# An encoder layer's instruction order, laid down by the other of the tile layer's two simulators

## Chip, cores and metric

The kernel runs on one core of a Trainium2 chip. The metric is the device time of one execution in microseconds; several runs give a median.

## The reference, cut to what matters

One encoder layer for 1024 tokens of width 2048, in float32. All products below are with weights of 512 to 4096 columns.

```python
def hybrid_layer(x, c, ...):
    mod = jax.nn.silu(c) @ w_ada + b_ada
    shift, scale, gate = jnp.split(mod, 3, axis=-1)
    h = rmsnorm(x, pre_g) * (1.0 + scale[:, None]) + shift[:, None]
    proj = h @ w_in                                   # 2048 -> 4608
    q, k, v, gate_a, u, gate_p = jnp.split(proj, SPLIT_POINTS, axis=-1)
    y_a = windowed_gqa(q, k, v, rel_table, sink) * jax.nn.silu(gate_a)   # 8 heads, blocks of 128, window 128
    y_p = multiscale_pool(u, w_pool_grp, pool_scale) * jax.nn.silu(gate_p)
    g = jax.nn.sigmoid(h @ w_merge + b_merge)         # 2048 -> 4096
    g_a, g_p = jnp.split(g, 2, axis=-1)
    merged = g_a * (y_a @ w_br_attn) + g_p * (y_p @ w_br_pool)
    o = merged @ w_out
    return x + gate[:, None] * rmsnorm(o, post_g)
```

## The kernel before

**Products.** Every large product is a Strassen scheme in Winograd's form: seven products of half-size blocks in place of eight. Each float32 operand is split into a rounded part and a remainder (`split`, L95 and L96: ScalarE writes the high part, VectorE the low one), and a product of two split operands is three matmuls (high by high, high by low, low by high). The moving operands, named `B11, T3, T2, B21, T4, T1, B22`, are made once from the activations and stay in SBUF for a whole pass: 7 names, 4 parts of the inner dimension, high and low, which is 56 tiles of 128x512, and the pool `big` has 56 slots. The weights come by DMA in pairs of 128 columns (`raw`, L187, four slots), are combined and split into rings of four (`whi`, `wlo`), and are used at once. The core of one product, in the function `strassen`:

```python
def product(wts, mov, ps, fresh=False):
    hi, lo = wts
    for n, (w_, m_) in enumerate(((hi, 0), (hi, 1), (lo, 0))):
        for i, j in enumerate(js):
            nc.tensor.matmul(ps, w_[:, i], op[mov][j][m_], ...)      # L235
```

A pair of weights goes through seven such products into three PSUM banks: X (with B11, then B21), V (T3, then T4) and Z (T2, T1, B22; it begins with a copy of X). With four parts of the inner dimension a product is 12 matmuls of 128x512 and a pair 84. Between the products ScalarE and VectorE read the banks (`u2` and `p7` at L245, `u4` at L290, additions at L102 and L105), and results go to DRAM (L311).

**Stages.**
1. Start: x and the first weights of the conditioning `w_ada` are loaded; rows are normalised and transposed by matmuls (`XT`, L405, with `turn`, L397), the shift and scale columns come from small matmuls (`GEMV`, L453). A first short set of pairs (the ramp) runs while the inner dimension's first half is still being made ready.
2. Pass 1: 34 pairs of `w_in` and `w_merge` for the first half of the inner dimension; partial sums go to `part_d`. Beside it run the rest of the conditioning (VectorE, L470), sums of the blocks of `w_out` (`weight_sums`, stored in `ws_d`), and the second half of h: rows of x (`xt`, L738 and L739) are scaled on ScalarE and transposed by matmuls (L745).
3. Pass 2: the same 34 pairs for the second half, with partial sums read back; results in `proj_d`. Beside it runs the attention in steps for 8 heads and 8 blocks of queries, two heads a step: scores (L849 to L851), softmax (L855 to L862), transposes (`PT`, L872) one step behind, values (`PV`, L882 to L884) two steps behind, gates at L836. Then the pooling branch (L928 to L976).
4. The branch products: 8 pairs for the attention branch, 8 for the pooling branch, with the gates (`gt`, L1074) and the sums of the two branches.
5. The output product (`out_pair`, matmuls at L1134 to L1136), in two halves of the tokens by two of the columns, and the final normalisation and residual (L1144 to L1156).

**Order.** The statements are traced by Python in one order: `run` steps through a pair's generator and puts steps of the side work between the products by hand (lists such as `every=(0, 2, 4, 6)`). The tile layer then makes the program. While it simulates the program, each engine takes, whenever it is free in the simulation, the earliest-written statement that is ready there, and slots of the pools are handed out as that goes on. That gives one list of instructions for each engine and for each queue of DMA issues (nearly all on SP's), with semaphores between them; on the chip each list runs in order. A few statements are tied to what was traced before them on their engine, by `tc.keep_in_program_order` (`keep`, and `pin` in `split`), and small writes to fresh slots (`claim`, L512) reserve them early.

## Time and profile before

| | us |
|---|---|
| median of 3 runs | 2147.35 (2147.01 to 2148.66) |
| the profiled execution | 2151.69 |
| its span, first to last instruction | 2149.9 |
| TensorE busy | 2100.2 |
| TensorE weight loads busy (beside the matmuls) | 1717.1 |
| VectorE busy | 1537.6 |
| ScalarE busy | 1129.0 |

The mean granted TensorE clock over the span is 0.996. Times inside the profile are microseconds from the first instruction. A busy time of TensorE counts matmuls that overlap in its pipeline once. L235 is line 235 of the kernel; a line can be that of a helper that many callers use, so operations are told apart by the names of the tiles.

### The profile page before, as it was taken

The page shows a single profiled execution, that of the slowest core. Times are in us where ns is not written, and L with a number is a line of the kernel's source. Part 1 is how long each engine was busy: PE and PEld are TensorE (multiplying, and loading weights), DVE is VectorE, ACT ScalarE, POOL GpSimd, SP SyncE. Part 2 cuts the span into 40 slices and gives each one's busy share as a digit, 9 for nine tenths or more (in the row PEclk, how much of TensorE's full clock was granted, in tenths as well). Part 3 has the DMA queues.
Part 4 walks back from the last instruction along what each step waited for, and adds up shares of the span by engine and source line. Part 5 has one row for each costly group of instructions (what it writes and reads, how often), then busy time and mean ns, then how long its engine had stood idle before and what let it go on. Part 6 is the DMA issues. An engine that isn't in the chain of part 4 may idle for free.

```text
span 2149.9 us, 28954 instructions
## 1 busy us (share of the span) xinstructions
PE 2100.2 (98%) x9567; PEld 1717.1 (80%) x9567; DVE 1537.6 (72%) x2754; ACT 1129.0 (53%) x2124; POOL 7.4 (0%) x66
## 2 busy tenths in 40 slices
PE   6999999999989999999999999999999999999998
PEld 3588888887878888888888888888788887878886
DVE  5786666786546676777776778666957967879667
ACT  5654444443464546767765433333645644667654
POOL 0000000000000000000000000000000000000000
PEclk9999999999999999999999999999999999999999
DMA  9986566998666446446454766765745655696997
GB/s 328 288 278 202 188 206 206 303 322 270 226 213 201 129 166 209 156 156 199 147 164 157 235 210 208 236 197 163 234 164 177 214 177 166 200 302 220 299 312 243
DMA packets 303255, 466.11 MB, mean 217 GB/s; under 512 B 23882, under 2 KB 144866, under 8 KB 303104
## 3 DMA queue, kind: packets, MB, share of 16 engines
q1 hardware_dynamic: 301648, 462.02, 66.0%
q0 software_dynamic: 1120, 2.19, 0.3%
q8 instruction: 75, 1.23, 0.2%
q14 instruction: 76, 0.62, 0.1%
q10 hardware_dynamic: 336, 0.06, 0.0%
HBM read 340.41 MB, written 125.85 MB: 217 GB/s over the span
## 4 chain that ended last, share of the span: by engine, by line
PE 85%; DMA 6%; DVE 5%; ACT 1%; issue 1%; SPq 0%; ACTq 0%; DVEq 0%; POOLq 0%
PE Z L235 29%; PE V L235 19%; PE X L235 19%; PE Z L1134 2%; PE Z L1135 2%; PE Z L1136 2%; PE V L1136 1%; PE V L1134 1%; PE V L1135 1%; PE GEMV L453 1%; DMA raw<-in_w_merge_dram 1%; DVE wlo L96 1%; PE X L1136 1%; PE X L1135 1%; PE X L1134 1%
## 5 line engine op out<-in xcount | busy, mean ns | idle before, releaser
L95 ACT ACTIVATE whi<-raw 128x512 fp32r<-128x512 f32 (+1 forms) x528 | 320.0, 609 | 501.4 <-PE Z L235 263.1
L96 DVE TENSOR_TENSOR wlo<-raw,whi 128x512 fp32r<-128x512 f32 (+1 forms) x528 | 346.6, 662 | 195.1 <-PE Z L235 119.2
L96 DVE TENSOR_TENSOR wlo<-wr,whi 128x512 fp32r<-128x512 f32 x224 | 151.1, 689 | 60.4 <-ACT whi L95 55.2
L95 ACT ACTIVATE whi<-wr 128x512 fp32r<-128x512 f32 x224 | 138.6, 629 | 92.5 <-DVE wlo L96 35.7
L102 DVE TENSOR_TENSOR raw<-raw,raw 128x512 f32<-128x512 f32 x80 | 55.2, 690 | 95.8 <-DMA raw<-in_w_merge_dram 71.1
L1074 ACT ACTIVATE gt<-gt,cols 128x512 f32<-128x512 f32 x64 | 45.9, 722 | 101.1 <-DMA gt<-proj_d 81.8
L235 PE MATMUL V<-T3h,whi 128*128 128x512 f32 x336 | 92.2, 393 | 3.9 <-DVE u L102 3.9
L235 PE MATMUL Z<-B22h,whi 128*128 128x512 f32 x336 | 93.8, 398 | 1.2 <-ACT u L290 1.2
L235 PE MATMUL X<-B11h,whi 128*128 128x512 f32 x336 | 92.4, 393 | 2.3 <-DVE part L102 1.0
L235 PE MATMUL Z<-T1h,whi 128*128 128x512 f32 x336 | 91.9, 392 | 0.9 <-ACT T1h L95 0.9
L235 PE MATMUL Z<-T2h,whi 128*128 128x512 f32 x336 | 92.3, 394 | 0.0
L235 PE MATMUL V<-T4h,whi 128*128 128x512 f32 x336 | 92.3, 393 | 0.0
L235 PE MATMUL Z<-B22l,whi 128*128 128x512 f32 x336 | 91.8, 393 | 0.0
L235 PE MATMUL Z<-T2l,whi 128*128 128x512 f32 x336 | 91.5, 393 | 0.0
L235 PE MATMUL X<-B11l,whi 128*128 128x512 f32 x336 | 91.3, 390 | 0.2 <-DVE B11l L96 0.2
L235 PE MATMUL Z<-B22h,wlo 128*128 128x512 f32 x336 | 91.4, 392 | 0.0
L235 PE MATMUL X<-B21h,whi 128*128 128x512 f32 x336 | 90.9, 390 | 0.0
L235 PE MATMUL V<-T4l,whi 128*128 128x512 f32 x336 | 90.9, 390 | 0.0
L235 PE MATMUL Z<-T1l,whi 128*128 128x512 f32 x336 | 90.8, 390 | 0.0
L235 PE MATMUL V<-T3l,whi 128*128 128x512 f32 x336 | 90.8, 390 | 0.0
L235 PE MATMUL Z<-T2h,wlo 128*128 128x512 f32 x336 | 90.8, 390 | 0.0
L235 PE MATMUL V<-T4h,wlo 128*128 128x512 f32 x336 | 90.8, 390 | 0.0
(306 smaller groups left out, 4848.2 us busy)
## 6 DMA issues: line engine op xcount, KB each, us to landing
part<-part_d SPq DMA_DIRECT2D x136, 256.0 KB, 5.0
ada<-in_w_ada_dram SPq DMA_DIRECT2D x128, 256.0 KB, 4.4
raw<-in_w_in_dram SPq DMA_DIRECT2D x64, 512.0 KB, 4.1
raw<-in_w_merge_dram SPq DMA_DIRECT2D x64, 512.0 KB, 5.6
wr<-ws_dS SPq DMA_DIRECT2D x64, 512.0 KB, 5.4
wr<-in_w_out_dram SPq DMA_DIRECT2D x48, 512.0 KB, 5.1
proj_d<-part SPq DMA_DIRECT2D x68, 256.0 KB, 2.2
sw<-in_w_out_dram SPq DMA_DIRECT2D x64, 256.0 KB, 5.1
```

The lines of the kernel that those rows point to most:

```text
L95: ins = (nc.scalar.activation(hi, src, AF.Copy), nc.vector.tensor_tensor(lo, src, f32(hi), ALU.subtract))
L96: nc.vector.tensor_tensor(lo, src, f32(hi), ALU.subtract))
L102: return (eng or nc.vector).tensor_tensor(o, a, b, ALU.add)
L235: nc.tensor.matmul(ps, w_[:, i], op[mov][j][m_], start=fresh and i == 0 and n == 0, stop=i == nj - 1 and n == 2, skip_group_check=True)
L453: ins = nc.tensor.matmul(pv[g:g + 32, :], scz[:, kc, :], tile_of(kc), start=kc < 4, stop=kc >= 12, tile_position=(0, g))
L1074: nc.scalar.activation(gt, gt, AF.Sigmoid, bias=cols[:, col:col + 1])
L1134: nc.tensor.matmul(pb, hi, w[0], start=first, stop=False, skip_group_check=True)
L1135: nc.tensor.matmul(pb, lo, w[0], start=False, stop=False, skip_group_check=True)
L1136: nc.tensor.matmul(pb, hi, w[1], start=False, stop=last, skip_group_check=True)
```

## The change

The tile context gets one more argument. Without it, the layer's scheduler decides which statement is ready by running the program in its plain simulator; with it, in its detailed timeline simulator, which follows the parts of an engine and the transfers as separate devices. Statements, tiles, pools, buffer counts and ties are the same.

```diff
     args.append(nc.dram_tensor("out_0_dram", (1, S, D), F32, kind="ExternalOutput").ap())
-    with tile.TileContext(nc) as tc:
+    with tile.TileContext(nc, schedule_with_timeline_sim=True) as tc:
         encoder_layer(tc, *args)
```

## The prediction

> **What bounds the kernel now.** I read the first two parts of the page first: which engine has no time left, and where.
>
> ```profile
> span 2149.9 us, 28954 instructions
> ...
> PE 2100.2 (98%) x9567; PEld 1717.1 (80%) x9567; DVE 1537.6 (72%) x2754; ACT 1129.0 (53%) x2124; POOL 7.4 (0%) x66
> ```
>
> TensorE (PE) is busy for 2100.2 of 2149.9 us, no other engine for more than 1537.6. So all that another order of the same instructions can win is 2149.9 - 2100.2 = 49.7 us of idle time, and what PE loses at a lower clock. The windows view says where these lie (columns: stretch, length, busy us of each engine with instructions in brackets, granted clock, DMA share, GB/s).
>
> ```profile
> 0.00:100.00 100.00, 78.89 (x387) 44.00 (x387) 62.28 (x156) 54.94 (x120) 3.94 (x46) 1.00 0.95 310
> 600.00:700.00 100.00, 94.20 (x433) 77.42 (x432) 57.63 (x92) 56.20 (x133) 0.00 (x0) 0.97 0.69 220
> 700.00:800.00 100.00, 100.00 (x443) 82.66 (x442) 72.23 (x116) 51.85 (x90) 0.00 (x0) 1.00 0.44 145
> 1500.00:1600.00 100.00, 98.61 (x431) 80.08 (x430) 80.79 (x130) 59.85 (x102) 0.00 (x0) 1.00 0.61 200
> 1600.00:1700.00 100.00, 100.00 (x441) 82.23 (x440) 77.11 (x123) 60.91 (x107) 0.00 (x0) 1.00 0.52 168
> 1800.00:1900.00 100.00, 96.44 (x410) 78.50 (x409) 80.65 (x129) 62.77 (x114) 0.00 (x0) 0.97 0.66 217
> 1900.00:2000.00 100.00, 98.71 (x433) 80.89 (x434) 85.25 (x145) 71.80 (x139) 0.00 (x0) 1.00 0.77 246
> 2100.00:2149.90 49.90, 40.96 (x181) 33.43 (x179) 36.34 (x63) 23.25 (x49) 0.00 (x0) 0.95 0.69 235
> ```
>
> The first stretch holds 100 - 78.89 = 21.1 us of the idle time, with the DMA engines at 0.95: that is the load of x and of the conditioning weights. The last holds 49.9 - 40.96 = 8.9 us, the final normalisation behind the last product. The 2000 us between hold the rest, 49.7 - 21.1 - 8.9 = 19.7 us, and half of that lies in two stretches, 600:700 (5.8) and 1800:1900 (3.6), the only two of these rows between the ends with a clock under 1. The PE rows of the waits view name the causes (columns: us in total, times, longest); these four hold 13 of the 19.7 us.
>
> ```profile
> PE b L745 <- ACT xt L739: 5.8, 2, 4.2
> PE V L235 <- DVE u L102: 3.9, 3, 1.7
> PE X L1134 <- DVE c L1085: 2.3, 1, 2.3
> ...
> PE PV L883 <- DVE pp L96: 1.0, 2, 0.6
> ```
>
> **What the change touches.** No instruction, size or buffer count changes. The tile layer lays down, before the run, the order of each engine's instructions: it simulates the program, and whenever an engine of the simulation is free, the earliest-written statement that is ready there goes next; slots of the pools are handed out in the same order. The chip then executes each engine's list strictly in that order. The change replaces the simulation that decides what is "ready". So each term below is an order that comes out otherwise, and I price it by what good and bad orders cost in the trace of before. Which orders come out can't be read from that trace; that is the main unknown.
>
> **The steady part: nothing.** Two products of the same name in successive weight pairs:
>
> ```profile
> 215.51 1.07 PE L235 MATMUL Z<-B22h,whi 128*128 128x512 f32 x4
> ...
> 234.55 1.07 PE L235 MATMUL Z<-B22h,whi 128*128 128x512 f32 x4
> ```
>
> They are 19.04 us apart; a pair is 7 products of 12 matmuls, so a matmul costs 19.04 / 84 = 0.2267 us and a product 2.72 us, without a wait. The split weights stand in rings of four (whi, wlo), the raw ones in four slots, so whoever schedules can't run far ahead and need not. How much disorder this absorbs is shown where it failed:
>
> ```profile
> 507.18 7.47 DMA raw<-in_w_merge_dram
> ...
> 515.99 5.28 DMA raw<-in_w_merge_dram
> ...
> 524.04 3.02 PE V L235 x12
> ```
>
> Here (the chain of waits) VectorE's list twice stood behind a weight load, 12.8 us together, and PE lost at most the 1.7 us of the longest "V <- DVE u" wait. So a wrong order on VectorE costs PE almost nothing until it blocks for about 12.8 - 1.7 = 11 us. I cost reordering of DVE, ACT and the SP queue inside the passes at zero; the cover is the rings of four, and without it every blocked us would be PE's.
>
> **The places without cover.** Two places show what PE pays when its own list has something too early (timeline of PE):
>
> ```profile
> 636.99 1.07 PE L235 MATMUL Z<-B22h,wlo 128*128 128x512 f32 x4
> 642.23 1.12 PE L745 MATMUL b<-ident,xt 128*128 128x128 f32 x4 [4.17 <-ACT xt L739]
> 643.00 2.06 PE L235 MATMUL Z<-T2h,whi 128*128 128x512 f32 x4
> ...
> 647.66 1.08 PE L235 MATMUL X<-B21h,whi 128*128 128x512 f32 x4
> ```
>
> From 636.99 to 647.66 are 10.67 us. The work in them is 16 matmuls of 0.2267 us, 3.63, and four transposes; the transposes take about 0.40 us at full rate (an estimate: 642.23 to 643.00, 0.77, at the rate seen there, 2.06 for four matmuls against 1.08). The loss is 10.67 - 3.63 - 0.40 = 6.6 us: 4.17 of waiting, 2.5 of a slower clock behind it. After the shorter wait at 524 the 12 matmuls took 3.02 against 2.72 us: no half rate. The Trainium skill ("TensorE: Matmul & The Clock Gate", Part 1) says the clock falls to half after an idle window of some 3.4 us and needs about as long a busy one to return; the trace agrees in kind (4.17 us did it, 1.7 did not), and by its figures the slow stretch would add an estimated 1.7 us instead of 2.5.
>
> ```profile
> 1822.45 1.07 PE L235 MATMUL Z<-T1h,wlo 128*128 128x512 f32 x4
> 1825.81 0.47 PE L1134 MATMUL X<-whi,mh 128*128 128x512 f32 x1 [2.29 <-DVE c L1085]
> ...
> 1828.59 2.08 PE L235 MATMUL Z<-B22h,whi 128*128 128x512 f32 x4 [0.56 <-ACT u L290]
> ...
> 1833.87 0.63 PE L1135 MATMUL X<-whi,ml 128*128 128x512 f32 x1
> ```
>
> Here the first matmuls of the output product (L1134) stand ahead of the last product of the branch (L235), and their bank is not free. From 1822.45 to 1833.87 are 11.42 us for 4 + 4 + 12 = 20 matmuls (four of L1134 to L1136 lie between the shown rows), 4.5 us at 0.2267: a loss of 6.9. So one entry that comes too early in PE's list costs about 7 us.
>
> Now the count. The stall at 642 comes from a load that landed later than the order supposed; a simulation that follows the transfers in more detail should put these transposes later: -6.6 us. The one at 1825 is a bank handed over by VectorE, no transfer; I leave it (0, at best -6.9). Against that stand four other handovers, at which the 56 slots of "big" pass from one moving operand to the next: into pass 2, into each branch, and between the halves of the output product. For the first three the view of the tile B11h gives the time of the first and last write.
>
> ```profile
> L95 ACT ACTIVATE B11h<-y x8: 614/616/635, 1496.5 to 1657.4; 128x512 fp32r<-128x512 f32 x8
> ...
> L95 ACT ACTIVATE B11h<-h x4: 615/619/634, 734.8 to 739.7; 128x512 fp32r<-128x512 f32 x4
> ```
>
> Pass 2 starts to fill at 734.8 us, the first branch at 1496.5, the second ends its first group at 1657.4; the fourth lies in 1900:2000. Each statement there takes a freed slot in the order in which the simulation finds it ready, and slots given to a later group keep an earlier one waiting. The windows 700:800, 1500:1600, 1600:1700 and 1900:2000 show that today they cost PE at most 0.00, 1.4, 0.00 and 1.3 us: there is little to win, and 6.6 us each to lose. Bounds for one: 0 (the order comes out alike), and 13.2 (two such stalls, head and tail of the handover). I take the middle, 6.6, the nearest measured stall: 4 x 6.6 = +26.4 us.
>
> The start: I take 0. DMA at 0.95 sets it; a 512 KB weight load moved ahead of x costs 0.5 MB / 310 GB/s = 1.7 us (an estimate from the first window), the order may win as much: -5 to +5 us for three of them. The tail: 0, bounds -2 and +4 (the 8.9 us are one chain behind the last product).
>
> Sum: -6.6 + 26.4 = +19.8 us. Against the profiled execution's 2151.69 us that is 2171.5; that one lay 4.3 us above the median of the runs, 2147.35, so the forecast is 2147.35 + 19.8 = **2167.2 us**. A difference of 0.2%, 4.3 us, is about what a measurement of this kernel can tell from none.
>
> **The rivals.** *Faster: the detailed simulation orders better.* One mechanism: entries that came too early go where their inputs have landed. Both 7 us stalls go (-6.6 - 6.9) and the stall at 524 (-1.7), the handovers stay free: 2147.35 - 15.2 = 2132.2. With the first alone it is 2140.8. For it: the three largest mid-span losses are of this kind. Against it: it can't win more than the 19.7 us of idle time and the slow clock of two windows, 2 x 100 x (1 - 0.97) = 6 us, so not reach below 2122. It decides as long as at most one of the four handovers comes out worse, since each that does gives back 6.6 us. Chance 0.26.
>
> *Much slower: the attention stage.* Behind the first pairs of pass 2, PE's list holds, between the products, the scores, transposes and values of 8 heads times 8 blocks, each behind a chain over ScalarE and VectorE.
>
> ```profile
> L836 ACT ACT_TABLE_LOAD x13 | 16.7, 1283 | 4.4 <-DMA g<-proj_d 4.2
> ```
>
> ScalarE loads a table for the gates 13 times here, 16.7 us, and must load the one of the softmax back each time; of these loads the detailed simulator by its own source takes no account. If it supposes these chains shorter than they are, PE's entries come too early, each time. PE's two waits for such a chain in the PV row are 0.5 us each; at two per block and head that is 64 x 2 x 0.5 = 64 us: with the 19.8 it is 2231.2. Against it: the transposes lag a step and the values two behind the scores in the statements, which the readiness rule doesn't shorten. Chance 0.18.
>
> *No change: both simulations find the same things ready.* The steady part, which is nearly all of PE's list, can't tell them apart; if the handovers come out alike too, it stays at 2147. Chance 0.09.
>
> **How the numbers follow.** The forecast (one to eight misplaced entries, 2152 to 2200) has 0.47, the attention rival 0.18 (2200 to 2250 and more), no change 0.09, faster 0.26. So slower has 0.65, same 0.09, faster 0.26. The range reaches from 2134, which leaves out the faster rival's best cases, a chance of about 0.1, to 2235, where the attention rival's upper half begins, about 0.09. The likeliest case's own range is 2152 to 2200.
>
> **What would show it.** In the profile after: PE busy us and instructions unchanged (2100 within some us, 9567), the pitch of 19.04 us kept in the passes; the difference is all in PE's idle time and in windows with a clock under 1. Right on the first term: no wait of "b L745 <- ACT xt" over 2 us. Right on the second: waits of 2 to 5 us on L235 or L1134 for splits (L95, L96) near the four handovers, windows there with 5 to 10 us less PE. The attention rival shows as many short waits on L849, L872 and L882 to L884. I am wrong if the steady passes themselves show gaps (then the rings aren't the cover I take them for), if the first 100 us move by more than 5 us, or if PE's busy time grows without idle time.

## The result and the profile after

| | before | after |
|---|---|---|
| median of 6 runs each, us | 2150.33 (2147.01 to 2154.39) | 2160.93 (2156.99 to 2163.40) |
| ratio of after to before | | 1.0049, 95% interval 1.0036 to 1.0061 |
| profiled execution / span, us | 2151.69 / 2149.9 | 2161.23 / 2159.4 |

The kernel is 10.6 us slower; 19.8 was forecast. The span grew by 9.5 us. The first lines of the page of after:

```profile
span 2159.4 us, 29009 instructions
...
PE 2105.6 (98%) x9567; PEld 1716.3 (79%) x9567; DVE 1534.0 (71%) x2754; ACT 1115.7 (52%) x2114; POOL 7.4 (0%) x66
```

TensorE runs the same 9567 matmuls and is busy 5.4 us longer (2100.2 before); its idle time grew by only 4.1 us, from 49.7 to 53.8. The windows view of after, for the stretches that the prediction showed (length, then busy us of PE, PEld, DVE, ACT, POOL, then granted clock, DMA share, GB/s):

```profile
0.00:100.00 100.00, 80.45 (x363) 41.50 (x363) 59.34 (x149) 52.34 (x114) 3.91 (x46) 1.00 0.95 311
600.00:700.00 100.00, 98.09 (x462) 80.48 (x462) 55.33 (x90) 60.06 (x147) 0.00 (x0) 1.00 0.69 216
700.00:800.00 100.00, 99.18 (x438) 81.83 (x437) 75.31 (x122) 52.70 (x91) 0.00 (x0) 1.00 0.48 156
1500.00:1600.00 100.00, 99.30 (x436) 81.35 (x436) 81.12 (x132) 60.19 (x102) 0.00 (x0) 1.00 0.61 205
1600.00:1700.00 100.00, 96.84 (x426) 79.56 (x425) 75.04 (x122) 59.72 (x102) 0.00 (x0) 1.00 0.48 161
1800.00:1900.00 100.00, 99.35 (x437) 81.52 (x436) 81.64 (x130) 63.26 (x114) 0.00 (x0) 1.00 0.68 221
1900.00:2000.00 100.00, 97.25 (x428) 79.90 (x427) 85.27 (x142) 72.11 (x139) 0.00 (x0) 1.00 0.72 240
2100.00:2159.40 59.40, 47.50 (x205) 37.80 (x203) 40.29 (x70) 26.80 (x57) 0.00 (x0) 0.93 0.64 220
```

The two weak stretches of before, 600:700 and 1800:1900, are mended: PE 98.09 and 99.35, clock 1.00. New are 1600:1700, where PE was full and now has 96.84, and the first row, where PE is busier (80.45 against 78.89) with fewer matmuls done (363 against 387). Of the PE rows of the waits view of after, behind those of the start (in us: total, times, longest):

```profile
PE V L235 <- DVE u L102: 4.0, 1, 4.0
PE Z L1134 <- ACT u L1216: 4.0, 4, 1.5
...
PE PT L872 <- DVE g L887: 2.3, 1, 2.3
PE V L235 <- ACT p L245: 2.1, 1, 2.1
...
PE b L745 <- ACT xt L739: 1.4, 2, 1.0
```

To see where the time came from I count the matmuls of the large products (L235 and L1134 to L1136; 8400 in both traces) and compare when the same number of them had started. The counts begin at 0, and the last row runs from the start of the last of these matmuls. At the chosen counts the work beside them is the same too. The last column holds the same stretch in the profiles of other kernels of the study whose lists there are as in before or as in after.

| stretch, by count of product matmuls | before, us | after, us | difference | other profiles with these lists |
|---|---|---|---|---|
| start to 120 (ramp) | 105.7 | 110.7 | +5.0 | before 104.8 to 106.0; after 110.2 |
| 120 to 1760 (pass 1, first half) | 376.0 | 382.8 | +6.8 | before 376.0 to 377.3; after 380.6 to 381.8 |
| 1760 to 2480 (pass 1, second half) | 188.3 | 180.8 | -7.5 | before 186.6 to 189.1; after 179.9 to 182.5 |
| 2480 to 3000 (into pass 2) | 118.0 | 119.0 | +1.0 | the same |
| 3000 to 5280 (attention, pooling) | 631.1 | 632.9 | +1.8 | before 628.0 to 634.9; after 634.3 to 635.3 |
| 5280 to 6360 (first branch) | 247.5 | 246.3 | -1.2 | before 247.6 to 248.0; after 246.4 to 246.6 |
| 6360 to 6960 (second branch) | 137.8 | 139.8 | +2.0 | before 137.6 to 139.2; after 141.0 to 141.1 |
| 6960 to 7160 (branch to output) | 52.7 | 46.6 | -6.1 | before 52.9 to 53.2; after 47.3 to 50.3 |
| 7160 to 8400 (output) | 283.6 | 289.1 | +5.5 | before 283.0 to 285.7; after 290.3 to 291.6 |
| last matmul to the end | 9.3 | 11.4 | +2.1 | before 9.1 to 9.7; after 11.3 to 11.4 |

The column of differences adds up to 9.5 with unrounded numbers. The change is thus ten differences of both signs, none over 8 us. "Loss" below means: in a stretch, the sum of the times from one matmul's start to the next, less the median of such steps of the same kind.

### The profile page after: what moved, and what is told of

It is laid out like the page before. It is cut to its first block, busy times and chain, and to the rows that moved or that the text cites. A ratio compares the mean times of both kernels' runs of the same rounds, so it can differ in the third digit from the quotient of the medians.

```text
span 2159.4 us, 29009 instructions
## 1 busy us (share of the span) xinstructions
PE 2105.6 (98%) x9567; PEld 1716.3 (79%) x9567; DVE 1534.0 (71%) x2754; ACT 1115.7 (52%) x2114; POOL 7.4 (0%) x66
## 4 chain that ended last, share of the span: by engine, by line
PE 82%; DMA 9%; DVE 5%; ACT 1%; issue 1%; SPq 0%; DVEq 0%; ACTq 0%; POOLq 0%
PE Z L235 27%; PE V L235 18%; PE X L235 18%; DMA xt<-in_x_dram 2%; PE Z L1134 2%; DMA raw<-in_w_merge_dram 2%; PE Z L1135 2%; PE Z L1136 2%; PE X L1134 1%; DVE wlo L96 1%; PE X L1135 1%; PE X L1136 1%; PE V L1136 1%; PE V L1135 1%; PE V L1134 1%
## 5 line engine op out<-in xcount | busy, mean ns | idle before, releaser
L96 DVE TENSOR_TENSOR wlo<-raw,whi 128x512 fp32r<-128x512 f32 (+1 forms) x528 | 347.7, 662 | 150.7 <-PE Z L235 96.1
L96 DVE TENSOR_TENSOR wlo<-wr,whi 128x512 fp32r<-128x512 f32 x224 | 150.2, 689 | 66.6 <-ACT whi L95 62.8
L102 DVE TENSOR_TENSOR raw<-raw,raw 128x512 f32<-128x512 f32 x80 | 55.3, 691 | 96.0 <-DMA raw<-in_w_merge_dram 64.4
L235 PE MATMUL V<-T3h,whi 128*128 128x512 f32 x336 | 93.4, 395 | 4.4 <-DVE u L102 4.0
L105 DVE TENSOR_TENSOR ws<-raw 128x512 f32<-128x512 f32 (+1 forms) x88 | 58.6, 666 | 54.1 <-DMA raw<-in_w_merge_dram 40.7
L235 PE MATMUL V<-T4h,whi 128*128 128x512 f32 x336 | 93.3, 393 | 2.1 <-ACT p L245 2.1
L235 PE MATMUL Z<-T1h,whi 128*128 128x512 f32 x336 | 91.9, 392 | 1.6 <-ACT u L245 1.6
L235 PE MATMUL V<-T3h,wlo 128*128 128x512 f32 x336 | 93.3, 394 | 0.0
L235 PE MATMUL V<-T3l,whi 128*128 128x512 f32 x336 | 93.1, 394 | 0.0
L235 PE MATMUL X<-B11h,whi 128*128 128x512 f32 x336 | 92.0, 392 | 1.0 <-DVE part L102 1.0
L235 PE MATMUL Z<-T1l,whi 128*128 128x512 f32 x336 | 92.0, 391 | 0.7 <-DVE T1l L96 0.7
L235 PE MATMUL Z<-B22h,whi 128*128 128x512 f32 x336 | 91.6, 392 | 1.1 <-ACT u L290 1.1
L235 PE MATMUL Z<-T1h,wlo 128*128 128x512 f32 x336 | 92.6, 391 | 0.0
L235 PE MATMUL X<-B21h,wlo 128*128 128x512 f32 x336 | 91.9, 390 | 0.0
L235 PE MATMUL Z<-T2h,wlo 128*128 128x512 f32 x336 | 91.9, 391 | 0.0
L235 PE MATMUL Z<-B22l,whi 128*128 128x512 f32 x336 | 91.9, 390 | 0.0
L235 PE MATMUL Z<-T2h,whi 128*128 128x512 f32 x336 | 91.9, 391 | 0.0
L235 PE MATMUL X<-B21h,whi 128*128 128x512 f32 x336 | 91.7, 390 | 0.0
L235 PE MATMUL Z<-T2l,whi 128*128 128x512 f32 x336 | 91.7, 390 | 0.0
L235 PE MATMUL Z<-B22h,wlo 128*128 128x512 f32 x336 | 91.5, 390 | 0.0
```

The source lines that it names most:

```text
L96: nc.vector.tensor_tensor(lo, src, f32(hi), ALU.subtract))
L102: return (eng or nc.vector).tensor_tensor(o, a, b, ALU.add)
L105: return nc.vector.tensor_tensor(o, a, b, ALU.subtract)
L235: nc.tensor.matmul(ps, w_[:, i], op[mov][j][m_], start=fresh and i == 0 and n == 0, stop=i == nj - 1 and n == 2, skip_group_check=True)
```

## The experiments

Theory: the difference is a sum of single places where an engine's list came out in another order, and each can be undone almost alone. Rival: the detailed order is slower as a whole, so that what is mended in one place comes back in another. "Tied" means an ordering on one engine without a wait on the chip (`add_manual_dep` of the kind NoSync). Each kernel was timed beside the kernel before, on the same chip; its ratio is to that. An edit makes the scheduler lay the lists anew, so each moves more than the entry meant: of TensorE's 9567 matmuls, about 3100 stand elsewhere with the tie of pass 1 on after and 403 with the same tie on before, and 5 to 292 with each other single edit.

**The ramp: conditioning products by fours.** Each of the 64 products of L453 uses 32 of TensorE's columns and leaves two matmul records (128 in both traces), so x2 below is one of them; the counts in the first expectation are of records. Timeline of PE in before:

```profile
77.26 1.05 PE L453 MATMUL GEMV<-ada,scz 128*32 128x512 f32 x4
...
79.84 1.05 PE L453 MATMUL GEMV<-ada,scz 128*32 128x512 f32 x4
```

and in after, where a product of the ramp is put between the two:

```profile
77.53 1.04 PE L453 MATMUL GEMV<-ada,scz 128*32 128x512 f32 x2
78.50 0.50 PE L235 MATMUL V<-T3h,wlo 128*128 128x512 f32 x1
78.94 1.04 PE L453 MATMUL GEMV<-ada,scz 128*32 128x512 f32 x2
```

Two side by side take 1.05 us, one alone 1.04. First edit, on after:

```diff
-            for kc in (2 * q, 2 * q + 1):
+            for kc in range(4 * q, 4 * q + 4) if pin else (2 * q, 2 * q + 1):
```

> The kernel after, with the conditioning products of the start (L453) written four to a step instead of two, so that four of 32 columns stand together in TensorE's list. Theory (the cost of the change is a sum of local entries of the lists): in after they stand two at a time, 1.04 us for two; in before four at a time, 1.05 us for four. Each group of four closed up saves about 1 us of TensorE's time, and the ramp up to 105 us gets back the 5 us that it lost: about -5 us in all, TensorE's busy time down by about as much, nothing else moved. Rival (the load sets the start): the DMA engines are at 0.95 of their time in the first 100 us, so TensorE would wait for weights instead: 0 us, busy time down by 5 us and idle time up by 5 us.

Measured: 2162.71 us, ratio 1.0050 (1.0032 to 1.0068): as after. Product 120 came at 109.95 us, and between 58 and 110 us ten groups still were x2: the scheduler went on giving each of the four its place as its own weights were ready. So the edit did not bring about what it was to test, and decides nothing. The second edit issues the four from the last loaded tile down:

```diff
+            for kc, tk in [(k, tile_of(k)) for k in range(4 * q, 4 * q + 4)][::-1] if pin else ...:
-                ins = nc.tensor.matmul(pv[g:g + 32, :], scz[:, kc, :], tile_of(kc), ...)
+                ins = nc.tensor.matmul(pv[g:g + 32, :], scz[:, kc, :], tk, ...)
```

> The kernel after with the conditioning products in fours, each four issued from the last loaded tile down, so that the first of a four waits for its last weights and the four stand together in TensorE's list (in the run with ascending order they had still come in twos). Theory (groups of four of 32 columns run side by side, groups of two take as long): about 8 pairs of 1 us saved between 70 and 100 us, the 40th to 120th product of pass 1 comes 4 to 5 us earlier, -4 us in all. Rival (the weights' arrival sets the ramp): the 120th product stays at 110 us within 1 us, 0 in all.

Measured: 2151.45 us, ratio 1.0005 (0.9991 to 1.0019), the time of before. From 69 us on the groups are fours; timeline of PE:

```profile
79.81 1.06 PE L453 MATMUL GEMV<-ada,scz 128*32 128x512 f32 x8
80.81 0.73 PE L235 MATMUL X<-B21h,whi 128*128 128x512 f32 x2
```

Product 120 starts at 99.1 us, 11.6 us earlier than in after. That is over twice the expectation, since fours also beat before's pairs. In its profile, which at 2156.81 us is a slow sample of this kernel, some of it is lost again at the end of the branches (stretch 6960 to 7160, 50.3 us against 46.6) and in the output. The rival falls: although the DMA engines are at 0.95 of their time there, TensorE's own work set the ramp. The busy time of L453 up to 110 us was 31.1 us in before, 37.7 in after and 25.7 here. The large products even start earlier in after, at 49.2 us with 22 conditioning products done, against 55.3 with 30 done in before; but from there to product 120 it is 61.5 us instead of 50.3.

**Pass 1: VectorE behind a weight load.** The chain of waits of after:

```profile
460.67 10.21 DMA raw<-in_w_merge_dram
...
470.98 0.69 DVE ws L105
471.67 0.61 DVE u L102
...
472.32 5.49 PE V L235 x12
```

VectorE's list has the first difference of the next pair (`ws`) ahead of the addition that frees bank V (`u`). From its issue the load took 10.21 us; VectorE stood for the last 5.10 of them, TensorE waited 4.0 us, and the next 12 matmuls took 5.49 us instead of 2.72. Edit, on after and on before:

```diff
-            sub(s3, a11, a21)
+            behind_v(sub(s3, a11, a21))
...
```

Here `behind_v` ties its instruction behind the latest addition out of bank V.

> The kernel after, with VectorE's first difference of the next weight pair (L260) put behind the addition that frees bank V. Theory (local): the wait of 4.0 us on V <- DVE u at 472 us and the half clock behind it, 7.2 us together, go: -7 us, 2154. Rival 1 (the load is late whatever the order): the weights that VectorE stood for took 10.21 us, and TensorE waits for the next pair's first product instead: 0 to -2 us. Rival 2 (the order as a whole is worse, not single entries): the list changes in many other places too, and new stalls of the same kind come up elsewhere: within 3 us of the kernel after, with the stall at 472 gone.

> The kernel before with VectorE's first difference of the next weight pair (L260) put behind the addition that frees bank V. Theory (the wait V <- DVE u is in before too: 1.5 us at 501 in its own profile, 4.4 to 5.3 us in other runs with the same order there, and 2 us at 522): no loss over 1 us at 495 to 530, -3 to -6 us in the median, 2147, and the runs scatter less than before's 2147 to 2160. Rival (the load behind it is late in any case): the wait moves to the split of the next pair and the time stays within 2 us.

On after: 2156.56 us, ratio 1.0024 (1.0012 to 1.0037), 4.4 us less than after by the medians and 5.4 by the ratios, between the theory and the second rival. The stall is gone; from product 120 to product 2480 pass 1 takes 556.3 us against 563.6, -7.3. In its profile 2.8 us of that go at the first branch (stretch 5280 to 6360) and 2.5 in the output, the first in lists that the tie changed, the second in lists that it did not. After's own profile also had the largest stall: the three other profiles with after's order at this place lost 5.0, 5.2 and 6.0 us there, about what the runs gained. On before: 2152.43 us, ratio 1.0005 (0.9993 to 1.0017), no gain: the rival's time. Nor do the runs scatter clearly less (12 runs from 2148.84 to 2157.44; before, 27 from 2145.35 to 2157.47). In its profile no loss between 495 and 530 us is left, and pass 1 takes 560.9 us where four profiles with before's lists take 562.9 to 565.2; of these 2 to 4 us the median shows nothing. So the local theory holds at its place in both kernels, but in the second its worth is not shown.

These runs also show how much luck is in one profile. VectorE's and SP's lists of this part are the same in before and in the three kernels below that differ from it at the handover near 1825 us. The loss at about 501 us was 1.5, 5.3, 4.9 and 6.3 us, as the load came. Before's own profile had the smallest.

**Output: two token rows apart.** The last matmuls of each output product are written for the first 128 tokens, then for the second. In after the two are interleaved to the end, so that both banks come free at once. ScalarE in before (timeline):

```profile
1897.54 0.60 ACT L1216 ACTIVATE u<-Z 128x512 f32<-128x512 f32 x1 [0.95 <-PE Z L1136]
1898.03 1.27 ACT L95 ACTIVATE whi<-wr 128x512 fp32r<-128x512 f32 x2
1899.21 0.58 ACT L1216 ACTIVATE u<-Z 128x512 f32<-128x512 f32 x1
```

ScalarE and TensorE in after:

```profile
1900.53 1.15 ACT L95 ACTIVATE whi<-wr 128x512 fp32r<-128x512 f32 x2 [1.76 <-PE Z L1136]
1901.59 1.07 ACT L1216 ACTIVATE u<-Z 128x512 f32<-128x512 f32 x2
```

```profile
1902.22 0.50 PE L1134 MATMUL Z<-whi,mh 128*128 128x512 f32 x1 [1.47 <-ACT u L1216]
```

Before copies the first row's bank under the second row's matmuls; after copies both at the end, and TensorE waits. Edit, on after: the first of the second row's last matmuls tied behind the last of the first row's, and likewise in the last product of all.

> The kernel after, with the second token row's last matmuls of each output product (L1134) tied behind the first row's last one, in the last product of all its matmuls. Theory (local): the four waits of Z <- ACT u (L1216), 4.0 us together, go, since ScalarE copies the first row's bank beside the second row's matmuls, and the tail behind the last matmul goes from 11.4 to 9.3 us: -6 us, 2155. Rival (the splits set the pace there): TensorE needs all the splits of a product sooner and waits for them (L95) instead: -2 us from the tail alone, or 0.

Measured: 2157.80 us, ratio 1.0026 (1.0012 to 1.0040). The gain against after is 3.1 us by the medians and 4.9 by the ratios; with intervals this wide it can be the 6 us of the theory or the 2 us of the rival. The tail is 8.7 us instead of 11.4, and no wait of Z for `u` (L1216) is left. In the middle part both theories have some right: waits for splits appeared (2.1 us of Z <- ACT whi, 1.4 of Z <- DVE wlo), and this profile's output stretch, 289.2 us, is no shorter than after's 289.1, though three other profiles of after's lists have 290.3 to 291.6. How much the middle part gains stays open.

**The transposes.** On before, each written a side step later:

```diff
-        if n >= 2:
-            turn_x((n - 2) // 2, n % 2, held.pop(n - 2))
+        if n >= 3:
+            turn_x((n - 3) // 2, (n - 3) % 2, held.pop(n - 3))
...
```

> The kernel before with the transposes of x for the scores (L745) written one side step later. Theory (they came too early for the load that they stand behind): no wait of b <- xt over 1 us, the losses at 598 to 617 and 622 to 647 us, 9.4 us together, fall to the 3.3 us that they are in after: -6 us, 2144.5. Rival (the load sets the pair, and another wait takes the place): the loss stays above 6 us, -3 us at most.

Measured: 2144.56 us, ratio 0.9966 (0.9953 to 0.9978), -7.3 us. The row "PE b L745 <- ACT xt" is no longer among its waits, and the two losses are 0.5 us each, less than after's 3.3 together. The mechanism that the prediction gave for this place is shown.

**The loss at 1825 us, three ways.** The prediction put it down to output matmuls that stand too early in TensorE's list. First edit, on before: the first output matmul tied behind the branch's last, its first split behind the branch's last split.

> The kernel before, with the first matmul of the output product (L1134) tied behind the last one of the branch (L235) and its first split behind the branch's last split; 18 lines of TensorE's list move, 8 of ScalarE's. Theory (one entry that comes too early in TensorE's list, with the slow clock behind it): the whole loss at 1825 us goes, -6.5 to -6.9 us, 2143.5. Rival (only the wait of 2.3 us hangs on the order, the low clock of that window on something else): -2.3 us, 2148, with the four matmuls of 2.08 us still there.

Measured: 2152.46 us, ratio 0.9999 (0.9985 to 1.0013). The loss there is 8.0 us instead of 7.3: both theories fall. TensorE now waits 5.5 us for the copy `u` of L290 in one piece. In before, ScalarE's timeline tells why:

```profile
1821.29 0.72 ACT L1074 ACTIVATE gt<-gt,cols 128x512 f32<-128x512 f32 x1 [3.53 <-DMA gt<-proj_d]
1821.92 1.13 ACT L95 ACTIVATE mh<-m 128x512 fp32r<-128x512 f32 x2
...
1826.90 0.63 ACT L95 ACTIVATE mh<-m 128x512 fp32r<-128x512 f32 x1 [2.80 <-DVE m L102]
1827.43 0.61 ACT L95 ACTIVATE whi<-wr 128x512 fp32r<-128x512 f32 x1
1827.95 0.58 ACT L290 ACTIVATE u<-Z 128x512 f32<-128x512 f32 x1
```

The sigmoid of a gate that only the last block needs holds ScalarE for 3.53 us; VectorE's sums wait for the splits behind it, the next split for those sums, and the copy for that split. Second edit: the first one, and the last split of the output operand written behind the copy.

> The kernel before with the tie of the run before (output matmuls behind the branch's last product), and besides with the last split of the output operand (L95, mh) written behind the copy of bank Z (L290), so that this copy no longer stands behind a split that waits for VectorE's sums on ScalarE. Theory now (the loss at 1825 us comes from ScalarE's list: the copy u <- Z of L290 waits behind mh <- m, that behind sums on VectorE, these behind a gate load of L1074): the copy comes at about 1824.5 instead of 1828, the loss there falls from 7.3 us (8.0 in the run before) to about 1.7, -5.5 us against the kernel before, 2145. Rival (the gate's load alone sets it, since it holds up ScalarE whatever stands behind it): 4 us or more stay lost, at most -3 us.

Measured: 2152.13 us, ratio 1.0003 (0.9994 to 1.0011). At the copy the loss fell to 2.0 us as the theory said, but 5.6 us were lost at 1830 to 1840, on VectorE's backlog (X <- DVE wlo, L96): 7.6 together. Third edit, on before alone: that gate's sigmoid issued behind the copy of L290.

> The kernel before with one gate moved: the sigmoid of the last block of the second branch (L1074) is issued behind the copy of bank Z (L290) instead of as soon as its load should be there. Theory (the loss at 1825 us begins with this sigmoid, which stands in ScalarE's list 3.5 us before its load has landed and holds up the splits of the output operand, the copy of bank Z and VectorE's sums behind them): the loss at 1823 to 1840 us, 7.3 us in before and 7.6 to 8.0 in the two runs that only moved what stands behind the gate, falls to 2 us or less: -5.5 us, 2146.5. Rival (VectorE's sums are late by themselves): another wait takes the place as in those two runs, 5 us or more stay lost.

Measured: 2147.03 us, ratio 0.9989 (0.9975 to 1.0004). Losses 2.1 and 1.4 us, 3.6 together; the stretch 6960 to 7160 takes 49.2 us against 52.7. In this profile half of the loss went with the gate; by the runs the gain is 2.4 us, and its interval holds 0. ScalarE's list of this kernel has a wait of 4.04 us for VectorE's sums at 1829 in its place. After has the gate in the same order too (a wait of 2.74 us), but 16 output matmuls ahead of the branch's last product, where before has four and the first edit none; the losses are 0.8 (up to 3.8 in other profiles of after's lists), 7.3 and 8.0 us. By that comparison, what the prediction called a matmul that comes too early is the filling of the gap, and there was too little of it. No edit changed the number of these matmuls alone, so this is argued and not shown.

**All together.** On after: the tie, the rows, the fours; and on both kernels the edits that had looked good.

> The kernel after with three edits together: the first difference behind the addition that frees bank V, the two token rows of the output products apart, the conditioning products in fours. Theory (the difference between the kernels is a sum of such entries): -4.4 of the first as measured, -3 of the second as measured, -4 of the third as expected: 2149.5, the time of before, within 3 us. Rival (each edit makes the scheduler lay other stalls elsewhere): 2155 or more.

> The kernel before with the tie of the difference, the transposes a step later and the last gate late. If the plain order's losses are single entries they add up: -7.5 as measured for the transposes, -3 to -6 for the tie, -5.5 for the gate: 2134. If the scheduler lays other stalls instead: 2142 or more.

> The kernel after with the three edits of the run that came to 2139.7, and the last gate late. There the loss at 1813 to 1829 is 1.3 us, so a gain of at most 1 us is to be expected if losses are local: 2139. If moving the gate lays stalls elsewhere: 2142 or more.

| kernel | median, us | ratio to before |
|---|---|---|
| after with tie, rows, fours | 2139.67 | 0.9947 (0.9934 to 0.9961) |
| the same and the last gate late | 2139.82 | 0.9951 (0.9934 to 0.9968) |
| before with tie, transposes, last gate late | 2142.56 | 0.9960 (0.9945 to 0.9976) |

The three edits on after gave 21.3 us by the medians; alone, by their ratios against 1.0049, they gave 5.4, 4.9 and 9.5, or 19.8. So on after, within what the intervals can tell, single entries do add up, and the version is about 12 us faster than before. The late gate added nothing to it (at most 1 us was expected). The page of the first:

```profile
span 2135.5 us, 28961 instructions
...
PE 2091.8 (98%) x9567; PEld 1715.0 (80%) x9567; DVE 1526.3 (71%) x2754; ACT 1107.8 (52%) x2120; POOL 7.4 (0%) x66
```

On before the run came out on the other branch of its expectation, 2142.6 instead of 2134, but because the parts were overrated: alone they measured +1.1 (tie), -7.3 (transposes) and -2.4 us (gate) by their ratios, -8.6 together, and 0.9960 is -8.6. The intervals of the two kinds overlap: with a few entries put right, neither simulator's order is shown to be the better one.

## Why the prediction was right or wrong

The direction, and the size within a factor of two, came out; of the terms, few did, and the direction was luck.

- **Steady passes, 0.** The pitch held (timeline of PE in after):

```profile
220.45 1.07 PE L235 MATMUL Z<-B22h,whi 128*128 128x512 f32 x4
239.49 1.07 PE L235 MATMUL Z<-B22h,whi 128*128 128x512 f32 x4
```

  19.04 us as before. But one gap of 7.2 us opened at 468 to 478, the sign that the prediction named as against it. The step that failed is the cover of about 11 us. The 12.8 us from which it was worked out are the lengths of two transfers in the chain of waits, not the time for which VectorE stood; that was 2.63 and 2.87 us (timeline of VectorE in before):

```profile
514.67 0.69 DVE L102 TENSOR_TENSOR raw<-raw,raw 128x512 f32<-128x512 f32 x1 [2.63 <-DMA raw<-in_w_merge_dram]
...
521.37 0.69 DVE L105 TENSOR_TENSOR ws<-raw 128x512 f32<-128x512 f32 x1 [2.87 <-DMA raw<-in_w_merge_dram]
```

  Only the second stands shortly ahead of the addition that frees bank V, and TensorE waited 1.71 of its 2.87 us. In after VectorE stood 5.10 us there (timeline of VectorE) and TensorE waited 4.05:

```profile
470.98 0.69 DVE L105 TENSOR_TENSOR ws<-raw 128x512 f32<-128x512 f32 x1 [5.10 <-DMA raw<-in_w_merge_dram]
```

  The cover at this place is thus about 1 us (2.87 - 1.71 and 5.10 - 4.05): the rings of four hold split weights, and the addition that frees bank V has no ring behind it. Over the whole of pass 1 after is still not slower (563.6 us against 564.3), since with before's lists 4.9 to 6.3 us were lost at 501 us in three of four profiles.
- **The transposes, -6.6.** As forecast: the longest wait for `xt` is 1.0 us, and the losses at these two places fell from 9.4 to 3.3 us, -6.0. With the other profiles of before's lists, which lost 5.9 to 7.0 there, it is more like -3. That a later place takes the loss away is shown by the edit on before (-7.3 us).
- **The loss at 1825, left at 0.** It went (-6.1). I kept it because VectorE and not a transfer hands over the bank; a transfer stood one engine further back, and half of the loss went with it in one profile. Reading the last releaser only, and not what stood before it in that engine's list, was the error.
- **Four handovers, +26.4.** +1.0 into pass 2, -1.2 at the first branch, +2.0 at the second, and between the output halves the only waits are two of the four for `u` (L1216), 2.7 us in 1900 to 2000, which come at the end of every output product. The mechanism shows once, at the second branch (timeline of PE in after):

```profile
1691.08 1.19 PE L235 MATMUL V<-T4h,whi 128*128 128x512 f32 x4 [2.10 <-ACT p L245]
...
1697.88 1.20 PE L235 MATMUL Z<-B22h,whi 128*128 128x512 f32 x4 [1.06 <-ACT u L290]
```

  These are waits for bank copies, not for the splits themselves. The first copy (L245) stands in ScalarE's list behind splits of the new operand, the second (L290) behind gates and a weight split. The size is what failed: 6.6 us each was the middle of bounds taken from the two worst places of the trace, and four places were priced as if they were certain to come out worse.
- **Start, 0 (-5 to +5).** +5.0, at the edge of the range and for another reason: I priced loads only, and the ramp's time was in how many of TensorE's small products run side by side. The windows of before in steps of 20 us could have told me: 16.3 of the 21.1 us of idle time lie in the first 20 us, and from 80 to 100 us TensorE is busy throughout.

```profile
0.00:20.00 20.00, 3.68 (x16) 3.46 (x17) 8.64 (x32) 11.59 (x29) 1.09 (x18) 1.00 0.82 279
...
80.00:100.00 20.00, 20.00 (x86) 11.28 (x82) 14.61 (x31) 12.78 (x26) 0.00 (x0) 1.00 0.72 225
```

  Over half of the net loss is here. Busy time that grows without idle time was a sign against the prediction; in the first 100 us it came (80.45 us busy against 78.89).
- **Tail, 0 (-2 to +4).** +2.1, within the bounds: both token rows finish at once.
- **Not in the sum:** the output stage but for its one handover, +5.5. The four waits for `u`, 4.0 us together, lie there, but the edit that removed them did not shorten the stage in its profile, so the cause of most of it stays open.

Of the rivals, the faster one had its two stalls right (-6.0 and -6.1), and its condition too, since no handover came out worse by anything near 6.6 us; the ramp and the output stage, which it did not have, turned the sign. The attention rival did not come: 631.1 to 632.9 us, within the scatter of before's own lists (628.0 to 634.9), longest wait 2.3 us.

So the forecast of slower was right through errors of both signs that cancelled. The four handovers stood in the sum at +26.4 and came to +1.8; the start, the output stage and the tail stood at nothing and came to +12.6; the stall at 1825 stood at nothing and came to -6.1; pass 1 without its transposes, and the attention, stood at nothing and came to +5.3 and +1.8.

## What to carry to other kernels

When a scheduler or its cost model is exchanged, compare the lists place by place, by a count of the same work: the total hides gains and losses that can be separated, and here three places put right were worth twice the difference. Look at three kinds of place: small matmuls that could run side by side and get something put between them; a statement that waits for a transfer and stands, on an in-order engine, ahead of one that frees a bank; and row orders written to stagger work. The length of a transfer in a chain of waits is not the time for which an engine stood; read that from the engine's own timeline. A stall of one profile that hangs on a transfer is a sample (1.5 to 6.3 us for the same lists), so price such terms from several.

## What the runs showed of the hardware

One, two and four products of 32 columns, written to four column groups and next to each other in the list, took 1.04, 1.05 and 1.06 us; a single full-width matmul between two of them costs the overlap. The Trainium skill ("TensorE: Matmul & The Clock Gate", Part 3) says that such tiles run concurrently for some 4 ns more each. The trace agrees, at 1.06 us for four.

The clock fell after a shorter wait than expected. In the profile of the first ramp edit the second branch's wait is as long as after's, 2.12 us, and yet the next matmuls ran at half rate (timeline of PE; after's 12 matmuls there took 1.19, 1.08 and 1.07 us for each four):

```profile
1688.92 1.67 PE L235 MATMUL V<-T4h,whi 128*128 128x512 f32 x4 [2.12 <-ACT p L245]
1690.39 1.91 PE L235 MATMUL V<-T4l,whi 128*128 128x512 f32 x4
1692.10 1.44 PE L235 MATMUL V<-T4h,wlo 128*128 128x512 f32 x4
```

The Trainium skill (the same page, Part 1) asks for an idle window of some 3.4 us; here 2.1 us did it in one execution and not in another. The clock records of the fourteen traces, from 100 us to 20 us before the end, show what decided. They hold 28 falls to half rate. Each slow stretch lasts 3.41 or 6.83 us, and within a trace the falls lie whole multiples of 3.413 us apart (470.88 and 1689.44 us in the profile above: 357 of them). If a trace is cut into such pieces, the wait of 2.12 us lies whole in one, and the next has half the clock, while after's wait of 2.10 us is split over two, 1.27 and 0.83 us (windows view, first of the ramp edit, then of after; the clock is the third number from the end):

```profile
1686.02:1689.44 3.42, 1.30 (x6) 0.79 (x5) 3.42 (x7) 3.33 (x7) 0.00 (x0) 1.00 0.76 217
1689.44:1692.85 3.41, 3.41 (x9) 2.64 (x9) 3.41 (x7) 1.25 (x3) 0.00 (x0) 0.50 0.89 286
```

```profile
1686.84:1690.25 3.41, 2.14 (x10) 1.44 (x8) 3.41 (x6) 3.02 (x6) 0.00 (x0) 1.00 0.50 173
1690.25:1693.66 3.41, 2.58 (x11) 2.16 (x12) 3.41 (x7) 2.24 (x5) 0.00 (x0) 1.00 1.00 311
```

Every piece before a fall holds 1.79 us or more of TensorE's idle time, and no other piece at full clock more than 1.91. So the prediction's two-sided reading (4.17 us did it, 1.7 did not) has its edge, in these traces, at about 1.8 to 1.9 us within one piece, and a stall of 2 us can cost 2 us or about 4 by where it falls.
